# A hybrid decoder layer on one core: the second norm in pairs of d tiles, the gate's first chunk fed pair by pair, the last norm on VectorE, and a smaller gather rate in the first half of the u product

## The chip, the cores and the metric

The kernel runs on one core of one Trainium2 chip. The metric is the device time of one execution in microseconds (us). Engines are named as in the profile: PE is TensorE, DVE is VectorE, ACT is ScalarE, POOL is GpSimd and SP is SyncE, which here only issues DMAs.

## The reference

One decoder layer with 256 tokens of 2048 columns: attention, an expert layer (PEER) that fetches 16 single-neuron experts for each of 8 heads of a token, and a gated embedding. Three layer norms follow the three residual sums. What bears on the change:

```python
def peer_ffn(x, wq, sub_keys, u, v):
    ...
        ub = u[eb]                                   # u, v: 16384 experts x 2048
        vbk = v[eb]
        act = gelu(einsum('thed,td->the', ub, xb))
        w = gb * act
        return einsum('the,thed->td', w, vbk)
...
x = layer_norm(alpha * x + mix_out, ln_g[i, 0], ln_b[i, 0])
ffn_out = peer_ffn(x, ...)
x = layer_norm(alpha * x + ffn_out, ln_g[i, 1], ln_b[i, 1])     # "second norm"
gate = sigmoid(einsum('bsd,de->bse', x, ple_gate[i]))           # 2048 x 2048
emb = einsum('bsk,kd->bsd', p[i], ple_proj[i])
x = layer_norm(alpha * x + gate * emb, ln_g[i, 2], ln_b[i, 2])  # "last norm"
```

## The kernel before, in words

**The expert layer.** 256 tokens are cut in two kinds. For 156 of them (`NDT`) the products with u and v run densely on TensorE over all 16384 experts, 128 blocks `ia` of 128 experts, each a weight load `wf` of 1 MB on SyncE's queue with `WF = 5` buffers. For the other 100 (`NSP`) the chosen rows are gathered: `gb` tiles of 128 rows by 2048 floats, fetched by indirect DMAs on GpSimd's queue (100 of `u_rows`, then 100 of `v_rows`) and used by VectorE (L841, L851). Dense blocks and gathers run side by side. `gathers(rate)` adds `rate` to a sum at every block and, for each whole one, issues one gather: a `mark` (a tiny DMA on SyncE's queue, L871, between the weight loads), a copy of it on GpSimd (`pace`, L872), and the gather (L874). So a gather can't start before the weight loads that stand ahead of its mark. The rates are `GU` for the first 64 blocks of u, `GUG` for the other 64, and `GV`, `GVG` for the two passes of v over halves of d (`dh` 0 and 1). What is left over of the 200 gathers is issued at the rate `GV` in the second pass of v, as long as there are any. `v` goes block by block in 16 matmuls.

**The gate stage** begins when the residual sums are transposed back (`res2`) and the statistics of both token tiles t (128 tokens each) are known (`stats2`, with rstd a power on GpSimd, L483). x2 is normalized, transposed in 128 x 128 tiles on TensorE (`ps_x2T`), multiplied by gain and bias per d tile on the way out of PSUM (`ln_cols`: even d tiles on VectorE, odd ones on ScalarE), and split in a high part (ScalarE's copy, L518) and a low part (VectorE's subtraction, L519), since a float32 product is made of three reduced ones: `mm3` (L222, L223, L224) is hi x wh, hi x wl, lo x wh. The weights `ple_gate` come in four chunks c of 512 columns, each as four loads, and are split in the same way, `wh` on ScalarE (L115) and `wl` on VectorE (L116), 16 pairs of 512 columns for a chunk: `parts0` (the first 8 pairs of chunk 0, split early) and `gate_parts`.

Before: `ln2(t)` normalizes all of a token tile, 512 columns at a time, alternating between VectorE (L1208) and ScalarE (L1206), then transposes four d tiles and makes X2 of `LB = 2` of them (128 columns of one token tile each). Token tile 0 is done whole, then half of tile 1, then the rest. The first chunk of the gate runs over the first half of d for both token tiles, then over the second.

`gate_out(c, t, ...)` takes a finished chunk: `em` (loaded by GpSimd's queue), sigmoid (L1234), times `em` (L1235), added to alpha x2 (L1236), and statistics (L1239). `natural_x2(c)` gives x2 its gain and bias in rows (loads of ln_g and ln_b, then two operations for each token tile on GpSimd, L1269 and L1270). `finish(t)` is the last norm: two passes over the columns on VectorE (L1247, L1255), with the last 448 or 320 columns on ScalarE and GpSimd (L1250 to L1252), each slice stored as it is done.

What sets the order: the Tile framework schedules the program and inserts the waits; instructions wrapped in `keep` hold the order in which they were written on their engine. Every engine works through its queue in that order, and a waiting instruction holds up what stands behind it.

Of the kernel before, what the change touches and what calls it, by code (L numbers as in the profile page):

```python
# [54 lines left out]
GU, GUG = 0.64, 0.75  # L55
# [8 lines left out]
LB = 2  # L64
# [99 lines left out]
def build(tc, a, out):  # L164
# [15 lines left out]
    half_neg = c0p.tile([P, 1], F32, name="half_neg")  # L180

# [37 lines left out]
    def mm3(ps, xt, k, t, wh, wl, start, stop):  # L219
        hi = xt[:, k, t * P:(t + 1) * P]  # L220
        lo = xt[:, k, T + t * P:T + (t + 1) * P]
        nc.tensor.matmul(ps, hi, wh, start=start, stop=False)  # L222
        nc.tensor.matmul(ps, hi, wl, start=False, stop=False)  # L223
        nc.tensor.matmul(ps, lo, wh, start=False, stop=stop)  # L224
# [276 lines left out]
    def ln_cols(dst, which, ps, d0, nd, n):  # L501

        for j in range(nd):
            dt = d0 + j
            g, b = gT[:, which, dt:dt + 1], bT[:, which, dt:dt + 1]
            if j % 2:
                nc.scalar.activation(dst[:, j, :], ps[:, j * n:(j + 1) * n], AF.Identity, bias=b,
                                     scale=g)
            else:
                nc.vector.tensor_scalar(dst[:, j, :], ps[:, j * n:(j + 1) * n], g, b,  # L510
                                        op0=ALU.mult, op1=ALU.add)

    def ln_T(pool, which, ps, d0, nd, c0, n):

        xx = pool.tile([P, nd, n], F32, name="ln_xx", tag="ln_xx", bufs=3)
        ln_cols(xx, which, ps, d0, nd, n)
        hi = X2[:, d0:d0 + nd, c0:c0 + n]
        nc.scalar.copy(hi, xx)  # L518
        return nc.vector.tensor_tensor(X2[:, d0:d0 + nd, T + c0:T + c0 + n], xx, hi.bitcast(F32),  # L519
                                       op=ALU.subtract)  # L520
# [679 lines left out]
    def ln2(t, d4s=range(ND // 4)):  # L1200
        if 0 in d4s:
            mv, rstd, nmr = stats2[t]
            for c in range(NCH):
                s = slice(c * 512, (c + 1) * 512)
                if c % 2:
                    nc.scalar.activation(x2[t][:, s], x2[t][:, s], AF.Identity, bias=nmr, scale=rstd)  # L1206
                else:
                    nc.vector.tensor_scalar(x2[t][:, s], x2[t][:, s], mv[:, 0:1], rstd,  # L1208
                                            op0=ALU.subtract, op1=ALU.mult)
        for d4 in d4s:  # L1210
            ps = pbank(pp, "ps_x2T")
            for j in range(4):
                dt = 4 * d4 + j
                nc.tensor.transpose(ps[:, j * P:(j + 1) * P], x2[t][:, dt * P:(dt + 1) * P], ident)
            for j in range(0, 4, LB):
                last = ln_T(l2, 1, ps[:, j * P:(j + LB) * P], 4 * d4 + j, LB, t * P, P)
        return last
# [8 lines left out]
    def gate_out(c, t, ps, c0, n):  # L1226
# [11 lines left out]
        for j in range(c0, c0 + n, 256):  # L1238
            nc.vector.bn_stats(st3[t][:, 2 * c + j // 256, :],  # L1239
                               x2[t][:, c * 512 + j:c * 512 + j + 256])  # L1240

    def finish(t, gr3, br3):
        mv, rstd, nmr = ln_stats(l2, st3[t], True)
        cut = [0, 512, 1024, D - (320 if t else 448), D]
        cs = [slice(*p_) for p_ in zip(cut, cut[1:])]
        for s in cs[:-1]:
            nc.vector.scalar_tensor_tensor(x2[t][:, s], x2[t][:, s], mv[:, 0:1], gr3[:, s],  # L1247
                                           op0=ALU.subtract, op1=ALU.mult)
        s = cs[-1]
# [163 lines left out]
```

## Time and profile before

| | |
|---|---|
| device time, median of 3 runs | 1786.87 us (1785.68 to 1787.45) |
| the profiled execution's own time | 1785.93 us |
| its span | 1784.2 us |
| granted TensorE clock | 0.998 |
| TensorE / VectorE / ScalarE / GpSimd busy | 98 / 60 / 31 / 30% |
| data moved | 606.23 MB, mean 340 GB/s |
| first half of u | about 532 to 806 us |
| statistics of the second norm | 1673 us |
| first and last gate matmul | 1679 and 1772 us |

Times in the profile are from the start of the span. A row of a group names line, engine, operation, the tiles (out<-in), shapes and count, then busy time, mean ns of one, and the idle time of the engine before them with what ended it. A row of a timeline gives the start, the length, and in brackets the engine's idle time before it with its releaser. A window gives for each engine the busy time in a stretch and the count of instructions. Some matmul records are missing from a trace.

### The profile page before, as it was taken

The page shows a single profiled execution, that of the slowest core. Times are in us where ns is not written, and L with a number is a line of the kernel's source. Part 1 is how long each engine was busy: PE and PEld are TensorE (multiplying, and loading weights), DVE is VectorE, ACT ScalarE, POOL GpSimd, SP SyncE. Part 2 cuts the span into 40 slices and gives each one's busy share as a digit, 9 for nine tenths or more (in the row PEclk, how much of TensorE's full clock was granted, in tenths as well). Part 3 has the DMA queues.
Part 4 walks back from the last instruction along what each step waited for, and adds up shares of the span by engine and source line. Part 5 has one row for each costly group of instructions (what it writes and reads, how often), then busy time and mean ns, then how long its engine had stood idle before and what let it go on. Part 6 is the DMA issues. An engine that isn't in the chain of part 4 may idle for free.

```text
span 1784.2 us, 30408 instructions
## 1 busy us (share of the span) xinstructions
PE 1755.0 (98%) x12074; PEld 1646.9 (92%) x12074; DVE 1064.5 (60%) x1706; ACT 546.5 (31%) x1363; POOL 530.9 (30%) x576
## 2 busy tenths in 40 slices
PE   8999999999999999999999999999999999999997
PEld 6888888888889999999999999999999999999786
DVE  5555589654698868455555544966433334333777
ACT  5677478733110100103333313652000000000552
POOL 0133033105346227232233332323233323220232
PEclk9999999999999999999999999999999999999999
DMA  7544644567998999999999999999999999998481
GB/s 283 191 165 166 235 143 154 195 239 253 381 418 311 421 416 416 421 421 419 420 419 410 418 419 413 404 418 399 421 421 420 421 421 420 416 411 341 167 298 65
DMA packets 99695, 606.23 MB, mean 340 GB/s; under 512 B 12824, under 2 KB 14672, under 8 KB 35648
## 3 DMA queue, kind: packets, MB, share of 16 engines
q1 hardware_dynamic: 67792, 387.91, 55.0%
q0 software_dynamic: 30320, 213.62, 29.3%
q10 hardware_dynamic: 1440, 2.75, 0.4%
q8 instruction: 95, 1.56, 0.4%
q14 instruction: 48, 0.39, 0.1%
HBM read 598.36 MB, written 6.03 MB: 339 GB/s over the span
## 4 chain that ended last, share of the span: by engine, by line
PE 89%; DMA 8%; DVE 2%; ACT 1%; issue 0%; SPq 0%; DVEq 0%; ACTq 0%
PE ps_v L1053 30%; PE ps_u L215 26%; PE ps_qk L203 7%; PE ps_q L215 6%; DMA wf<-peer_u 5%; PE ps_qk L205 3%; PE ps_v L223 2%; PE ps_v L224 2%; PE ps_v L222 2%; PE ps_gate L223 1%; PE ps_gate L222 1%; PE ps_gate L224 1%; PE ps_mix L223 1%; PE ps_mix L224 1%; PE ps_mix L222 1%; DMA wf<-peer_v 1%
## 5 line engine op out<-in xcount | busy, mean ns | idle before, releaser
L1053 PE MATMUL ps_v<-A,wf 128*128 128x156 f32 x4096 | 551.9, 297 | 0.8 <-DMA wf<-peer_v 0.8
L1053 PEld LDWEIGHTS ps_v<-A,wf 128*128 128x128 f32 x4096 | 544.5, 190 | 1.8 <-DMA wf<-peer_v 1.3
L215 PE MATMUL ps_u<-XF,wf 128*128 128x156 f32 x3904 | 531.5, 297 | 5.9 <-DMA wf<-peer_u 4.5
L215 PEld LDWEIGHTS ps_u<-XF,wf 128*128 128x128 f32 x3904 | 519.6, 190 | 10.0 <-ACT A L986 5.6
L851 DVE SCALAR_TENSOR_TENSOR y<-gb,ew,y 128x2048 f32<-128x2048 f32 x94 | 220.8, 2349 | 222.0 <-DMA gb<-v_rows,eig 221.8
L841 DVE SCALAR_TENSOR_TENSOR gb<-gb,xq 128x2048 f32<-128x2048 f32 x100 | 231.5, 2319 | 147.7 <-DMA gb<-u_rows,eig 147.7
L116 DVE TENSOR_TENSOR wl<-wf,wh 128x1024 fp32r<-128x1024 f32 (+1 forms) x199 | 213.3, 1095 | 99.0 <-ACT wh L115 97.2
L872 POOL COPY pace<-mark 1x1 f32<-1x1 f32 x200 | 116.4, 582 | 513.9 <-DMA mark<-c_iota 513.4
L115 ACT CAST wh<-wf 128x1024 fp32r<-128x1024 f32 (+1 forms) x199 | 171.8, 893 | 151.3 <-PE ps_yn L897 39.8
L203 PE MATMUL ps_qk<-X,wh 128*128 128x512 f32 x512 | 185.2, 401 | 0.0
L986 ACT ACTIVATE A<-ps_u 128x156 f32<-128x156 f32 x128 | 38.4, 300 | 442.9 <-PE ps_u L215 357.0
L874 POOL DMA_INDIRECT gb<-u_rows,eig x100 | 114.7, 1147 | 143.7 <-DVE gb L841 74.7
L874 POOL DMA_INDIRECT gb<-v_rows,eig x100 | 123.4, 1234 | 78.4 <-DVE y L851 39.0
L205 PE MATMUL ps_qk<-X,wl 128*128 128x256 f32 x512 | 145.7, 285 | 0.0
L939 ACT ACTIVATE hi<-eq,ghf 128x64 f16<-128x64 f16 x312 | 104.5, 335 | 40.6 <-DVE eq L933 35.9
L203 PEld LDWEIGHTS ps_qk<-X,wh 128*128 128x128 f32 x512 | 96.4, 188 | 21.9 <-issue 1.0
L215 PE MATMUL ps_q<-XF,wf 128*128 128x256 f32 x512 | 113.6, 379 | 0.6 <-DVE XF L510 0.6
L1114 ACT COPY x<-ps_y 128x256 f32<-128x256 f32 (+3 forms) x12 | 5.2, 439 | 350.0 <-DVE st L1113 349.8
L215 PEld LDWEIGHTS ps_q<-XF,wf 128*128 128x128 f32 x512 | 95.9, 190 | 13.1 <-DVE XF L510 0.8
L940 ACT ACTIVATE lo<-eq,glf 128x64 f16<-128x64 f16 x312 | 104.1, 334 | 0.0
L205 PEld LDWEIGHTS ps_qk<-X,wl 128*128 128x128 f32 x512 | 96.3, 188 | 2.5 <-issue 1.3
L957 DVE SCALAR_TENSOR_TENSOR A<-ps_G,A 128x30 f32<-128x30 f32 (+2 forms) x96 | 32.6, 368 | 38.0 <-PE ps_G L947 21.9
(261 smaller groups left out, 1836.1 us busy)
## 6 DMA issues: line engine op xcount, KB each, us to landing
wf<-peer_v SPq DMA_DIRECT2D x128, 1024.0 KB
wf<-peer_u SPq DMA_DIRECT2D x122, 1024.0 KB
wf<-w_qk SPq DMA_DIRECT2D x64, 512.0 KB
wf<-w_out SPq DMA_DIRECT2D x32, 512.0 KB
wf<-peer_wq SPq DMA_DIRECT2D x16, 1024.0 KB
wf<-ple_gate SPq DMA_DIRECT2D x16, 1024.0 KB
wf<-w_v SPq DMA_DIRECT2D x31, 512.0 KB
early<-peer_u SPq DMA_DIRECT2D x6, 1024.0 KB
```

Source lines behind the costliest of these rows:

```text
L115: self.order(nc.scalar.copy(wh, src))
L116: self.order(nc.vector.tensor_tensor(wl, src, wh.bitcast(F32), op=ALU.subtract))
L203: nc.tensor.matmul(ps, wh[:, j * P:(j + 1) * P], xt[:, dt, :], start=dt == 0, stop=False)
L205: nc.tensor.matmul(ps[:, :T], wl[:, j * P:(j + 1) * P], xt[:, dt, :T], start=False, stop=dt == ND - 1)
L215: nc.tensor.matmul(ps[:, :T - t0], wf[:, dt * P:(dt + 1) * P], xt[:, dt, t0:], start=dt == 0, stop=dt == ND - 1)
L841: keep(nc.vector.scalar_tensor_tensor(g, g, 1.0, xq[i], op0=ALU.mult, op1=ALU.mult, accum_out=eact[i][:, j:j + 1]))
L851: keep(nc.vector.scalar_tensor_tensor(ys[i], g, ew[i][:, j:j + 1], ys[i], op0=ALU.mult, op1=ALU.add))
L872: keep(nc.gpsimd.tensor_copy(pace, mark))
L874: keep(nc.gpsimd.indirect_dma_start(out=g, out_offset=None, in_=a[kind], in_offset=bass.IndirectOffsetOnAxis(ap=eig[i][:, 0, j:j + 1], axi ...
L939: nc.scalar.mul(hi[:, j, :], eq[:, j, :], ghf[:, t])
L940: nc.scalar.mul(lo[:, j, :], eq[:, j, :], glf[:, t])
L1053: return nc.tensor.matmul(ps[:, (j % 2) * NDT:(j % 2 + 1) * NDT], vf[:, j * P:(j + 1) * P], W_of(ia), start=False, stop=ia == NIA - 1 and ...
```

## The change

Four things are edited.

1. `GU` goes from 0.64 to 0.60.
2. The second norm: `ln2_norm(c)` normalizes 512 columns of token tile 0 on VectorE and of token tile 1 on ScalarE. `ln2_pair(d2)` transposes two d tiles for both token tiles (four transposes in one PSUM bank) and makes X2 of 256 columns for each. All of it is wrapped in `keep`.
3. The gate's first chunk: for each pair of d tiles, the norm if the pair is even, the pair's X2, up to two weight splits, then the twelve matmuls of the pair before (`gate_pair`). `natural_x2(0)` with its loads stands behind `pace2`, a copy on GpSimd that reads X2 of d tile 13. The first eight splits of chunk 1 are written ahead of the last pair's matmuls.
4. The last norm: all columns on VectorE, in slices of 512 for token tile 0 and of 640, 640, 512 and 256 for token tile 1; token tile 0's is written ahead of the last half chunk's output. All stores are issued by SyncE.

```diff
-GU, GUG = 0.64, 0.75
+GU, GUG = 0.60, 0.75
...
-    def ln2(t, d4s=range(ND // 4)):
...
+    def ln2_norm(c):
+        s = slice(c * 512, (c + 1) * 512)
+        (mv, rstd, _), (_, rstd1, nmr1) = stats2
+        keep(nc.vector.tensor_scalar(x2[0][:, s], x2[0][:, s], mv[:, 0:1], rstd,
+                                     op0=ALU.subtract, op1=ALU.mult))
+        keep(nc.scalar.activation(x2[1][:, s], x2[1][:, s], AF.Identity, bias=nmr1, scale=rstd1))
+
+    def ln2_pair(d2):
+        d = slice(2 * d2, 2 * d2 + 2)
+        ps = pbank(pp, "ps_x2T")
+        for j in range(2):
+            for t in range(NT):
+                c0 = (2 * d2 + j) * P
+                keep(nc.tensor.transpose(ps[:, j * T + t * P:j * T + (t + 1) * P],
+                                         x2[t][:, c0:c0 + P], ident))
+        xx = l2.tile([P, 2, T], F32, name="ln_xx", tag="ln_xx", bufs=2)
+        ln_cols(xx, 1, ps, 2 * d2, 2, T, keep)
+        hi = X2[:, d, :T]
+        keep(nc.scalar.copy(hi, xx))
+        keep(nc.vector.tensor_tensor(X2[:, d, T:], xx, hi.bitcast(F32), op=ALU.subtract))
...
+    def finish(t, mv, rstd, cut):
+        cs = [slice(*p_) for p_ in zip([0] + cut, cut + [D])]
+        for s in cs:
+            keep(nc.vector.scalar_tensor_tensor(x2[t][:, s], x2[t][:, s], mv[:, 0:1], gr3[:, s],
+                                                op0=ALU.subtract, op1=ALU.mult))
+        for s in cs:
+            keep(nc.vector.scalar_tensor_tensor(x2[t][:, s], x2[t][:, s], rstd, br3[:, s],
+                                                op0=ALU.mult, op1=ALU.add))
             nc.sync.dma_start(out[t * P:(t + 1) * P, s], x2[t][:, s])
-
-    ln2(0)
-    ln2(1, range(ND // 8))
...
-    parts = [parts0, gate_parts(0, 1)]
-    ln2(1, range(ND // 8, ND // 4))
+    gw = [sg.load(a["ple_gate"][0, i]) for i in range(2, 4)]
+    pss = [pbank(pa, "ps_gate") for _ in range(NT)]
+
+    def gate_pair(d2):
+        for k in range(2 * d2, 2 * d2 + 2):
+            for t in range(NT):
+                mm3(pss[t], X2, k, t, *parts0[k], k == 0, k == ND - 1, keep)
+
+    for d2 in range(ND // 2):
+        if d2 % 2 == 0:
+            ln2_norm(d2 // 2)
+        ln2_pair(d2)
+        if d2 > 1 and len(parts0) < ND:
+            parts0.append(sg.split(gw[(len(parts0) - 8) // 4], len(parts0) % 4 * 512))
+        if d2 > 3 and len(parts0) < ND:
+            parts0.append(sg.split(gw[(len(parts0) - 8) // 4], len(parts0) % 4 * 512))
+        if d2 > 0:
+            gate_pair(d2 - 1)
+    keep(nc.gpsimd.tensor_copy(pace2, X2.bitcast(F32)[0:1, ND - 3, 0:1]))
+    natural_x2(0, nc.gpsimd)
     for t in range(NT):
         keep(nc.scalar.copy(em3[:, t], pse[t]))
-    pss = [pbank(pa, "ps_gate") for _ in range(NT)]
-    for half in range(2):
-        for t in range(NT):
-            gate_mm(pss[t], t, parts[half], 0, 512, half * ND // 2)
-        if not half:
-            natural_x2(0, nc.gpsimd)
+    first = gate_parts(1, 0)
+    gate_pair(ND // 2 - 1)
     for c in range(NCH):
         if c == NCH - 1:
+            finish(0, *mr0, [512, 1024, 1536])
             gate_out(c, 1, ps_half, 256, 256)
+            finish(1, *finish_stats(1), [640, 1280, 1792])
             break
         gate_out(c, 0, pss[0], 0, 512)
-        first = gate_parts(c + 1, 0)
+        if c:
+            first = gate_parts(c + 1, 0)
         gate_out(c, 1, pss[1], 0, 512)
         parts = first + gate_parts(c + 1, 1)
         natural_x2(c + 1, nc.sync)
...
         gate_out(c + 1, 0, pss[0], 0, 512)
+        mr0 = finish_stats(0)
         gate_out(c + 1, 1, pss[1][:, :256], 0, 256)
         ps_half = pss[2][:, :256]
-    for t in range(NT):
-        finish(t, gr3, br3)
```

More of the change, by code (lines that the diff above doesn't have):

```diff
@@ L63 @@
 WF = 5
-LB = 2
 class Pools:
@@ L180, in build @@
     half_neg = c0p.tile([P, 1], F32, name="half_neg")
+    pace2 = c0p.tile([1, 1], F32, name="pace2")
     xap = pools.open("xap", "left", bufs=1)
@@ L506, in ln_cols @@
             if j % 2:
-                nc.scalar.activation(dst[:, j, :], ps[:, j * n:(j + 1) * n], AF.Identity, bias=b,
-                                     scale=g)
-            else:
[L510 to L520, printed above, removed]
+                order(nc.scalar.activation(dst[:, j, :], ps[:, j * n:(j + 1) * n], AF.Identity,
+                                           bias=b, scale=g))
+            else:
+                order(nc.vector.tensor_scalar(dst[:, j, :], ps[:, j * n:(j + 1) * n], g, b,
+                                              op0=ALU.mult, op1=ALU.add))
     def ln_rows(pool, which):
```

56 lines of the change are left out of this document (16 added, 40 removed).

## The prediction

> **What bounds the kernel now.** I read the page first, then windows of the first half of the u product, then GpSimd's timeline there, then the groups and timelines of the last 115 us. The page:
>
> ```profile
> PE 1755.0 (98%) x12074; PEld 1646.9 (92%) x12074; DVE 1064.5 (60%) x1706; ACT 546.5 (31%) x1363; POOL 530.9 (30%) x576
> PE 89%; DMA 8%; DVE 2%; ACT 1%; issue 0%; SPq 0%; DVEq 0%; ACTq 0%
> ```
>
> TensorE is busy 98% of the span, and the chain that ends last is TensorE for 89% and a DMA for 8%. So only two kinds of time can move: the few microseconds in which TensorE waits, and what follows its last matmul. A reader should not take the other engines' shares as slack: in the gate stage they set when TensorE starts.
>
> Windows of two views (stretch, length, then busy time and count for each engine, granted clock, DMA share, GB/s):
>
> ```profile
> core 0: us, PE busy (x) PEld busy (x) DVE busy (x) ACT busy (x) POOL busy (x), PEclk, DMA share, GB/s
> 600.00:620.00 20.00, 20.00 (x153) 20.00 (x152) 17.94 (x58) 1.60 (x6) 5.03 (x8) 1.00 1.01 419
> 620.00:650.00 30.00, 29.37 (x214) 28.29 (x214) 15.91 (x44) 2.10 (x7) 7.02 (x9) 1.00 1.02 414
> 720.00:770.00 50.00, 46.76 (x341) 45.00 (x340) 22.57 (x26) 7.27 (x18) 13.90 (x15) 1.00 1.01 421
> 795.00:806.00 11.00, 10.32 (x76) 9.91 (x75) 8.37 (x11) 2.08 (x9) 2.11 (x3) 1.00 1.02 424
> 840.00:860.00 20.00, 18.74 (x151) 18.07 (x150) 14.01 (x20) 8.24 (x34) 7.17 (x9) 1.00 1.02 422
> 1606.00:1636.00 30.00, 30.00 (x228) 30.00 (x228) 14.54 (x13) 3.74 (x7) 3.50 (x4) 1.00 0.98 393
> 1636.00:1656.00 20.00, 20.00 (x141) 18.93 (x140) 4.39 (x9) 2.18 (x4) 0.00 (x0) 1.00 0.62 216
> ```
>
> An unstalled u stretch runs 152 or 153 matmuls in 20 us, 0.132 us each; a u block has 32 of these records, 4.2 us. By that pace the four u windows lack 14, 39, 8 and (by idle time) about 10 matmuls: 1.8, 5.1, 1.0 and 1.3 us. The DMA share is 1 in all of them: TensorE waits there because a weight load shares full DMA engines with expert gathers. At 421 GB/s one load, 1.05 MB, takes 2.5 us; a gather (128 rows of 2048 floats) has the same size.
>
> ```profile
> 723.85 0.96 POOL L874 DMA_INDIRECT gb<-u_rows,eig  x1 [4.61 <-DVE gb L841]
> 738.78 0.96 POOL L874 DMA_INDIRECT gb<-u_rows,eig  x1 [3.83 <-DVE gb L841]
> 741.11 0.18 POOL L872 COPY pace<-mark 1x1 f32<-1x1 f32 x1 [1.37 <-DMA mark<-c_iota]
> ```
> ```profile
> L874 POOL DMA_INDIRECT gb<-v_rows,eig x100: 956/958/3097, 1020.0 to 1613.8; - x100
> ...
> DMA to landing us min/median/max: 5.5/12.3/22.5
> ```
>
> Until 739 GpSimd issues a gather every 4.98 us (the first and the last of four stand here) and waits for VectorE to free a buffer, not for a mark: it works off a backlog of marks. At 741 it waits for a mark for the first time, so only from there does GU set the rate.
>
> **Fewer gathers (GU 0.64 to 0.60).** Over the 64 u blocks of the first half 2.56 gathers go, 6.4 us of DMA time. In the new order of SyncE's queue one mark fewer has been issued by block 20 to 26, and two by block 45 (about 725 us). The first stall (620 to 650) falls into the backlog, where marks do not count: it stays. In the window from 720 to 770 TensorE got 39 matmuls too few, 1.2 blocks at 32 matmuls, so 1.2 loads or 3 us of DMA time; two gathers fewer give 5. I take that stall and the one at 795 as nearly gone: -5.5 of 6.1 us. Bounds: -1.5 (the backlog only shortens and the loads gain no turn before 750) and -8 (the stall at 840 goes too, and some of the first). The 2.56 gathers come later, behind the last v gather, which was issued at 1613.8: v makes 0.35 of a gather for every 16 matmuls (2.1 us), so they take 7.3 such steps, 15.5 us; the last is issued about 1629 and lands, at the median of 12.3, about 1641. The DMA share is 0.98 to 1636 and 0.62 behind it, which takes them: +0.3, up to +2 if the last of them hold up the residual sums in which they are added.
>
> **The gate's first chunk.** Its durations, from the groups of 1672 to 1785 and from the two lines of `ln_cols` (min/median/max ns, the 256-column form is the one after the change):
>
> ```profile
> L222 PE MATMUL ps_gate<-wh,X 128*128 128x512 f32 x112 | 43.4, 393 | 3.4 <-ACT X L518 3.4
> L116 DVE TENSOR_TENSOR wl<-wf,wh 128x512 fp32r<-128x512 f32 x56 | 35.2, 697 | 0.1
> L115 ACT CAST wh<-wf 128x512 fp32r<-128x512 f32 x56 | 29.8, 619 | 0.0
> L1270 POOL TENSOR_TENSOR x<-x,XF 128x512 f32<-128x512 f32 x8 | 13.2, 1673 | 0.0
> L1269 POOL TENSOR_TENSOR x<-x,XF 128x512 f32<-128x512 f32 x8 | 10.3, 1308 | 44.6 <-DMA XF<-ln_g 44.6
> ...
> L1234 ACT ACTIVATE sig<-ps_gate 128x512 f32<-128x512 f32 x7 | 4.2, 599 | 33.5 <-PE ps_gate L224 33.5
> L1206 ACT ACTIVATE x<-x,ln_nmr,ln_rstd 128x512 f32<-128x512 f32 x4 | 3.0, 807 | 0.1
> L1208 DVE TENSOR_SCALAR x<-x,ln_mv,ln_rstd 128x512 f32<-128x512 f32 x4 | 2.0, 551 | 0.6 <-POOL ln_rstd L483 0.6
> ```
> ```profile
> L510 DVE TENSOR_SCALAR XF<-ps_x1T,gT,bT x8: 534/535/546, 411.2 to 418.7; 128x256 f32<-128x256 f32 x8
> L507 ACT ACTIVATE XF<-ps_x1T,bT,gT x8: 556/564/598, 412.8 to 419.2; 128x256 f32<-128x256 f32 x8
> ```
> ```profile
> 1673.92 1.19 POOL L483 TENSOR_TENSOR ln_rstd<-ln_rstd,half_neg 128x1 f32<-128x1 f32 x2 [59.19 <-DVE ln_rstd L482]
> ```
> ```profile
> 1679.53 0.60 PE L1214 MATMUL ps_x2T<-ident,x 128*128 128x128 f32 x4
> ```
> ```profile
> 1705.36 0.59 ACT L1234 ACTIVATE sig<-ps_gate 128x512 f32<-128x512 f32 x1
> ...
> 1727.55 0.60 ACT L1234 ACTIVATE sig<-ps_gate 128x512 f32<-128x512 f32 x1 [1.45 <-PE ps_gate L224]
> ```
>
> The last three fences are of GpSimd's, TensorE's and ScalarE's timelines. The sigmoids at 1705.36 and 1727.55 mark the ends of chunks 0 and 1: 22.2 us for 96 matmuls, so one costs 0.2275 and chunk 1 now loses 0.35. A pair of d tiles has 12 matmuls, 2.73 us, and four transposes, 0.60 from the first to the last result and so 0.11 each in the pipeline, 0.44: 3.17 us of TensorE. Its chain on the other engines is serial, since the program lets ScalarE's half of `ln_cols` wait for VectorE's and the copy for both: the transposes and the hand-over 0.64, then 0.58, 0.60, 0.66 and 0.62, each a row above with 0.04 for the hand-over or less its overlap with what follows. The program puts the next norm behind all that on both engines, behind the weight splits of the pair too, and TensorE's queue has the transposes of every second pair waiting for that norm, with 12 matmuls of the pair before standing behind them. So from the transposes of an even pair to those of the next: 3.17 + 0.64 + 2.46, plus 0.62 for each weight split, plus 0.59 for the norm: 7.5 us with one split, 8.1 to 8.6 with two, against 6.34 of TensorE.
>
> In numbers: both rstd by 1675.11, the norm of token tile 1 on ScalarE (0.29 and 0.81) done by 1676.3, transposes 1676.4, X of pair 0 ready 1678.9. Its matmuls end 1681.8; the norm for pairs 2 and 3 ends 1682.5 (stall 0.6); next transposes at 1690.0 (stall 1.1) and 1698.3 (1.9); then 0.44 + 0.44 + 3 x 2.73 of work and 0.4 for the pipeline: chunk 0 ends about 1707.7 instead of 1705.3. So **+2.4**. It keeps the first wait and trades the other of the two that make up the 3.4 us of L222 for three smaller ones. Bounds: -1.6 (nothing but the first wait), +5.5 (each split delays the norm by both engines' rows).
>
> **Chunk 1.** `natural_x2(0)` moves from the start of the stage to behind `pace2`, which waits for ScalarE's copy of pair 6. On GpSimd's queue the loads of `em` for chunk 0 stand behind it.
>
> ```profile
> 1686.56 1.14 POOL L1230 DMA_DIRECT2D em<-s_emb  x2
> ```
> ```profile
> 1709.75 0.68 DVE L1235 TENSOR_TENSOR sig<-sig,em 128x512 f32<-128x512 f32 x1
> 1710.53 0.69 DVE L1236 SCALAR_TENSOR_TENSOR x<-x,sig 128x512 f32<-128x512 f32 x1
> 1711.26 0.75 DVE L1239 BATCH_NORM_STATS2 st<-x 128x6 f32<-128x256 f32 x2
> ...
> 1721.99 1.79 DVE L1235 TENSOR_TENSOR sig<-sig,em 128x512 f32<-128x512 f32 x1 [5.18 <-ACT sig L1234]
> ```
> ```profile
> em<-s_emb POOLq DMA_DIRECT2D x6, 256.0 KB, 3.5
> ...
> XF<-ln_g POOLq DMA_DIRECT2D x1, 256.0 KB, 5.9
> ```
>
> Copy of pair 6 at 1700.8, pace 0.5, ln_g issued 1701.3, landed 5.9 later: 1707.2. Four operations of 1.31 and 1.67 each twice: 1713.2. `em` issued there, landed 3.5 later: 1716.7. On VectorE the two outputs of chunk 0 now stand between the first and the second eight splits of chunk 1: wl of tile 8 comes after 2 x (0.69 + 0.69 + 0.75) = 4.3, with 0.7 of its own at 1721.7. TensorE needs it 49 matmuls into chunk 1, at 1718.9. That is 2.8 us of stall; the GpSimd operations of `natural_x2(1)` now run in the same stretch, and one VectorE operation beside such a one took 1.79 instead of 0.68. I add half a meeting: **+3.3**. Bounds: 0 (both loads land in half the time) and 7 (all four meet).
>
> The Trainium skill's page "SBUF — State Buffer", section "Who interferes with whom", says that VectorE and GpSimd take one shared port pair as an exclusive lock, for a whole instruction. By that rule up to four meetings, 4.4 us, would come on top of 2.8 here, 7.2 instead of 3.3; the row of 1.79 agrees with a wait of most of one GpSimd operation.
>
> **Chunk 2.** In the new order of TensorE the first token tile of chunk 1 ends 6 matmuls before the chunk does (1.36 us; 27, or 6.1 us, before). Its output now stands ahead of the splits of chunk 2 on both engines. Sigmoid 0.6, 0.69, 0.69, 0.75, a split 0.7 and two hand-overs make 3.5; less 1.36 and one matmul, TensorE stands 1.9 us. With half a meeting with GpSimd: **+2.5**, bounds 1.9 and 4. Chunk 3 keeps 28 matmuls of distance: nothing. The 0.35 that chunk 1 loses now is part of these: -0.35.
>
> **Tail.**
>
> ```profile
> 1772.00 0.38 ACT L1234 ACTIVATE sig<-ps_gate 128x256 f32<-128x256 f32 x1 [3.63 <-PE ps_gate L224]
> ```
> ```profile
> 1773.16 0.41 DVE L1235 TENSOR_TENSOR sig<-sig,XF 128x256 f32<-128x256 f32 x1
> ...
> 1775.06 2.27 DVE L1247 SCALAR_TENSOR_TENSOR x<-x,ln_mv,g_row 128x512 f32<-128x512 f32 x3
> 1777.24 3.47 DVE L1255 SCALAR_TENSOR_TENSOR x<-x,ln_rstd,b_row 128x512 f32<-128x512 f32 x3
> ```
>
> VectorE starts the last product 1.2 us behind the last matmul and ends 8.7 behind it. After: it has eight passes of 512 for tile 0 instead of six, free of GpSimd. The first token tile of chunk 3 now ends 72 short matmuls ahead of the last, 8.5 us at 0.118; its output, the statistics and the first half of tile 1's output take 5.1 of these, so the passes start 3.4 ahead of the last matmul and 8 x 0.66 ends 1.9 behind it. Then 1.9 to the passes as now, and twice 2048 columns at 2.27/1728 us per column, 5.4: 9.2 in all, +0.5; the last store has 256 columns and lands some 0.3 to 0.5 earlier. **0**, bounds -0.7 and +1.
>
> **Sum.** 2.4 + 3.3 + 2.5 - 0.35 = +7.9 in the gate; -5.5 in u; +0.3 in v: +2.7. The profiled execution took 1785.93 (span 1784.2), so 1788.6 by its own time; the median of the runs shown, 1786.87, lies 0.9 above it, so **1789.5**. A difference of 0.2%, 3.6 us, is about what a measurement of this kernel can tell from none: 1783.3 to 1790.4 counts as the same.
>
> **Rivals.**
> (a) The gate runs at TensorE's pace: the norms do get done between the splits, and chunk 1 meets no late `em`. Its place is chunk 0's wait at every even pair; it decides if the chain of a pair with norm and splits is under 6.34 us instead of 7.5. Then the gate gives -1.6 and the whole -1.6 - 5.5 + 0.3: 1780, faster. Against it stand the rows of the chain; for it, that PE's total work is unchanged. Chance 0.15.
> (b) GpSimd's loads land sooner than the rows say: two of each alone, not beside weight loads. If ln_g and `em` together take 3.3 us less, chunk 1's stall is gone: 1786.2, no change. Chance 0.17.
> The page "DMA: Bandwidth & Descriptors" of the Trainium skill, section "Anatomy of one DMA — SWDGE (gpsimd) path", gives 2.0 us plus the bytes at 436 GB/s for a DMA on this path, an estimate of 2.6 us here. That would be 4.2 us less in the two landings; the rows of 5.9 and 3.5 speak against it in this stage.
> (c) The gathers free nothing: the loads' stall returns at the next place because the DMA engines stay full anyway. For it: the share is 1 in every window of u, and a transfer that is only moved does not leave the queue shorter. Then 1789.5 + 5.5 = 1795, slower. Chance 0.20.
> (d) The late gathers hold the last residual sums and the stage starts 3 us later: 1792.5. Chance 0.06.
> The forecast itself, 1786.5 to 1793, has 0.42.
>
> **How the numbers follow.** Leaving out most of (a) below and the far ends of (c) above, the range is 1781 to 1796. Faster: (a) 0.15 and the lower ends of forecast and (b), 0.07: 0.22. Same: most of (b) and the lower half of the forecast: 0.36. Slower: 0.42.
>
> **What would show it.** Right: u windows of 720 to 770 with 375 or more matmuls; three waits of ps_x2T for VectorE or ScalarE, growing; `em` landing after 1715; a wait of ps_gate L223 (the wl matmul) in the middle of chunk 1 and at the start of chunk 2. Wrong: the sigmoids of chunk ends 22 us apart, or the u window with 341 matmuls as now.

## The result and the profile after

The changed kernel takes 1798.07 us (median of 4 runs, 1796.77 to 1799.64), the kernel before 1787.16 beside it: ratio 1.0063, 95% interval 1.0045 to 1.0080. It is slower by some 11 us; the forecast was 1789.5 in a range from 1781 to 1796.

The profiled execution has a span of 1795.0 instead of 1784.2, 10.8 us more. From the starts of TensorE's matmuls in both traces the difference divides as follows. u goes from its first start to its last, the next stretch to the last start of the matmuls of `ps_emb`, behind which the second norm begins. A chunk of the gate is counted by 96 matmuls of 512 columns (two of 256 count as one), from its first start to the next chunk's.

| stretch | before | after | difference |
|---|---|---|---|
| up to the first u matmul | 531.79 | 532.84 | +1.05 |
| u | 567.17 | 560.42 | -6.75 |
| v, residual sums, statistics | 575.52 | 577.11 | +1.59 |
| to the first gate matmul | 4.47 | 4.27 | -0.20 |
| gate chunk 0 | 25.95 | 29.28 | +3.33 |
| gate chunk 1 | 22.45 | 28.35 | +5.90 |
| gate chunk 2 | 21.98 | 27.36 | +5.38 |
| gate chunk 3 | 22.36 | 22.42 | +0.06 |
| last start of a matmul to the end of the span | 12.47 | 12.95 | +0.48 |

Nothing ahead of u is edited; its 1.05 is how executions differ (u starts between 531.8 and 534.8 in the fourteen traces of this case). So u gains what was forecast and a little more, and the gate stage loses 14.5 us instead of 7.9.

TensorE's waits (tile and line, what it waited for: us in all, times, longest), two rows of the kernel before and then the changed kernel, whose line numbers differ (its L115 is the kernel before's L116):

```profile
PE ps_u L215 <- DMA wf<-peer_u: 4.5, 13, 0.5
PE ps_gate L222 <- ACT X L518: 3.4, 2, 1.7
```
```profile
PE ps_gate L223 <- DVE wl L115: 6.9, 4, 3.3
...
PE ps_x2T L1206 <- DVE x L1195: 3.4, 3, 2.0
PE ps_v L1044 <- DMA wf<-peer_v: 2.3, 3, 1.0
PE ps_gate L222 <- ACT X L1211: 1.4, 1, 1.4
PE ps_u L215 <- DMA wf<-peer_u: 1.2, 3, 0.5
```

Before, the gate's matmuls waited 3.4 us, all in chunk 0 and for X. Now the largest group is a wait for `wl`, VectorE's half of the weight split, and waits for loads of `peer_u` fell from 4.5 to 1.2. The windows of u and two in the gate stage (PE busy and count first; the last three columns are clock, DMA share and GB/s):

```profile
620.00:650.00 30.00, 29.24 (x213) 28.08 (x212) 17.03 (x46) 1.81 (x6) 7.44 (x10) 1.00 1.02 414
720.00:770.00 50.00, 48.90 (x366) 48.20 (x365) 18.76 (x22) 7.16 (x18) 10.72 (x13) 1.00 1.01 420
795.00:806.00 11.00, 11.00 (x91) 10.97 (x91) 5.49 (x9) 3.49 (x15) 3.00 (x5) 1.00 1.02 419
840.00:860.00 20.00, 20.00 (x176) 19.96 (x175) 10.55 (x15) 7.05 (x31) 7.88 (x7) 1.00 1.01 419
...
1712.00:1720.00 8.00, 6.98 (x21) 4.67 (x21) 7.76 (x9) 0.38 (x1) 5.72 (x5) 0.79 0.62 204
1738.00:1746.00 8.00, 8.00 (x29) 6.31 (x29) 7.86 (x15) 2.50 (x5) 0.00 (x0) 0.80 0.87 312
```

The first stall stays (213 matmuls against 214), the window from 720 to 770 has 366 matmuls instead of 341, the stalls at 795 and 840 are gone. In the last two windows the granted clock falls to 0.8, which it did nowhere in the kernel before between the first matmul of u and the last of the gate.

Where the time of chunk 1 goes is read from VectorE's and GpSimd's timelines side by side (start, length, count; the line's idle time and releaser in brackets), and from the landing of the two loads of `em` that GpSimd issues at 1709.2. VectorE:

```profile
1697.72 1.29 DVE L115 TENSOR_TENSOR wl<-wf,wh 128x512 fp32r<-128x512 f32 x2
...
1702.24 13.34 DVE L115 TENSOR_TENSOR wl<-wf,wh 128x512 fp32r<-128x512 f32 x8 [0.80 <-ACT wh L114]
1715.51 1.76 DVE L1230 TENSOR_TENSOR sig<-sig,em 128x512 f32<-128x512 f32 x1
...
1720.94 4.89 DVE L115 TENSOR_TENSOR wl<-wf,wh 128x512 fp32r<-128x512 f32 x8
1731.74 1.11 DVE L1230 TENSOR_TENSOR sig<-sig,em 128x512 f32<-128x512 f32 x1 [5.91 <-ACT sig L1229]
1732.96 1.58 DVE L1231 SCALAR_TENSOR_TENSOR x<-x,sig 128x512 f32<-128x512 f32 x1
1734.57 0.75 DVE L1234 BATCH_NORM_STATS2 st<-x 128x6 f32<-128x256 f32 x2
1735.24 5.18 DVE L115 TENSOR_TENSOR wl<-wf,wh 128x512 fp32r<-128x512 f32 x8
```

GpSimd:

```profile
1697.14 0.71 POOL L1285 COPY pace<-X 1x1 f32<-1x1 f32 x1 [26.16 <-ACT X L1211]
1697.80 0.63 POOL L1260 DMA_DIRECT2D XF<-ln_g  x1
...
1702.40 1.70 POOL L1262 TENSOR_TENSOR x<-x,XF 128x512 f32<-128x512 f32 x1 [3.40 <-DMA XF<-ln_g]
...
1709.19 1.14 POOL L1225 DMA_DIRECT2D em<-s_emb  x2
1710.34 1.29 POOL L1262 TENSOR_TENSOR x<-x,XF 128x512 f32<-128x512 f32 x1
...
1715.11 1.61 POOL L1263 TENSOR_TENSOR x<-x,XF 128x512 f32<-128x512 f32 x1
```

The loads of `em` (view of the tile from 1709 to 1710), and TensorE's wait for `wl` of tile 8, the first of the second eight splits, 50 matmuls into chunk 1:

```profile
DMA to landing us min/median/max: 5.1/5.1/5.1
```
```profile
1721.67 0.50 PE L223 MATMUL ps_gate<-wl,X 128*128 128x512 f32 x1 [1.51 <-DVE wl L115]
```

The eight operations of the natural rows of chunks 0 and 1 run from 1702.4 to 1716.7, one behind the other. In the same stretch VectorE makes the first eight splits of chunk 1, and they take 13.3 us: the first, begun before GpSimd, takes 0.69 us, the other seven 1.77 to 2.48 each. The next eight, with GpSimd idle, take 4.9 together. `sig` times `em` then starts at 1715.5 with no idle time before it: `em`, issued at 1709.2, had landed at 1714.3 and was not waited for, but by only 1.3 us.

### The profile page after: what moved, and what is told of

It reads as the page before. It is cut to its first block, busy times and chain, and to the rows that moved or that the text cites. A ratio compares the mean times of both kernels' runs of the same rounds, so it can differ in the third digit from the quotient of the medians.

```text
span 1795.0 us, 30354 instructions
## 1 busy us (share of the span) xinstructions
PE 1759.3 (98%) x12074; PEld 1648.1 (92%) x12074; DVE 1065.3 (59%) x1692; ACT 541.6 (30%) x1343; POOL 535.2 (30%) x573
## 3 DMA queue, kind: packets, MB, share of 16 engines
q0 software_dynamic: 30320, 213.62, 29.2%
## 5 line engine op out<-in xcount | busy, mean ns | idle before, releaser
L115 DVE TENSOR_TENSOR wl<-wf,wh 128x1024 fp32r<-128x1024 f32 (+1 forms) x199 | 220.9, 1131 | 110.8 <-ACT wh L114 99.0
L863 POOL COPY pace<-mark 1x1 f32<-1x1 f32 x200 | 107.0, 535 | 517.1 <-DMA mark<-c_iota 516.5
L865 POOL DMA_INDIRECT gb<-u_rows,eig x100 | 127.5, 1275 | 129.6 <-DVE gb L832 68.7
L215 PEld LDWEIGHTS ps_q<-XF,wf 128*128 128x128 f32 x512 | 95.9, 190 | 13.1 <-DVE XF L510 0.8
L223 PE MATMUL ps_gate<-wl,X 128*128 128x512 f32 (+1 forms) x144 | 54.2, 381 | 6.9 <-DVE wl L115 6.9
```

Of the source, the lines that this page charges most:

```text
L115: self.order(nc.vector.tensor_tensor(wl, src, wh.bitcast(F32), op=ALU.subtract))
L215: nc.tensor.matmul(ps[:, :T - t0], wf[:, dt * P:(dt + 1) * P], xt[:, dt, t0:], start=dt == 0, stop=dt == ND - 1)
L863: keep(nc.gpsimd.tensor_copy(pace, mark))
L865: keep(nc.gpsimd.indirect_dma_start(out=g, out_offset=None, in_=a[kind], in_offset=bass.IndirectOffsetOnAxis(ap=eig[i][:, 0, j:j + 1], axi ...
```

## The experiments

Each run stands beside runs of the kernel before on the same chip; the table has the medians and the ratios, and the chunk times are counted as above. Kernels are compared by what each lies above or below its own before: the changed kernel +10.9.

| run | us | before | ratio (95%) | chunks 0, 1, 2, 3 | half clock in the gate, us (chunk) |
|---|---|---|---|---|---|
| changed kernel | 1798.07 | 1787.16 | 1.0063 (1.0045 to 1.0080) | 29.3, 28.4, 27.4, 22.4 | 3.4 (1), 3.4 (2) |
| GU alone | 1780.43 | 1786.16 | 0.9971 (0.9960 to 0.9983) | 25.9, 22.5, 22.0, 22.4 | none |
| all but GU | 1805.59 | 1786.16 | 1.0119 (1.0102 to 1.0136) | 29.3, 28.3, 28.3, 22.4 | 6.8 (1), 6.8 (2) |
| no natural rows in 0 and 1 | 1789.93 | 1786.16 | 1.0024 (1.0013 to 1.0036) | 29.3, 22.1, 23.4, 22.4 | none |
| no pace2 | 1793.18 | 1786.16 | 1.0043 (1.0027 to 1.0060) | 34.6, 22.1, 22.8, 22.4 | 6.8 (0) |
| norms ahead | 1796.82 | 1785.91 | 1.0070 (1.0053 to 1.0087) | 27.8, 28.2, 27.2, 22.4 | 3.4 (0), 3.4 (2) |
| splits ahead | 1791.70 | 1785.91 | 1.0035 (1.0022 to 1.0047) | 29.2, 27.7, 22.1, 22.4 | none |
| no natural rows in 1 | 1796.51 | 1785.91 | 1.0068 (1.0051 to 1.0085) | 31.5, 24.0, 28.4, 22.4 | 6.8 (0), 6.8 (2) |
| last norm alone | 1787.00 | 1785.91 | 1.0008 (0.9998 to 1.0018) | 25.7, 22.5, 22.0, 22.4 | none |
| norms and splits ahead, no pace2 | 1790.23 | 1785.52 | 1.0023 (1.0013 to 1.0033) | 32.9, 22.5, 22.1, 22.4 | 6.8 (0) |
| norms and splits ahead | 1788.24 | 1785.52 | 1.0015 (1.0006 to 1.0025) | 26.7, 29.3, 22.1, 22.4 | 3.4 (1) |
| the same, rows 1 to 3 held | 1799.30 | 1786.23 | 1.0075 (1.0058 to 1.0091) | 26.7, 26.5, 25.0, 29.9 | 3.4 (1), 6.8 (3) |
| GU 0.56 alone | 1788.34 | 1786.23 | 1.0010 (1.0000 to 1.0019) | 25.8, 22.3, 22.0, 23.1 | none |

The chunk times are those of one traced execution of each kernel. The last column says how long TensorE's granted clock was 0.5 in it during the gate, and in which chunk: a matmul then starts 0.427 us behind the one before instead of 0.2275, so 3.4 us of it cost 1.6 us of TensorE's time, unless TensorE would have waited for something else anyway. Differences of one or two us between chunk times are to be read with it.

**GU alone**, in the kernel before.

```diff
-GU, GUG = 0.64, 0.75
+GU, GUG = 0.60, 0.75
```

> The kernel before with GU at 0.60 and nothing else. Theory A (the u and v parts of the changed kernel's trace are GU's doing and the gate stage is separate): u ends some 6 us earlier, v gives back some 1.5 by the gathers moved behind it, and the time is about 5 us lower, 1782; the gate stage keeps its 92.7 us from first to last gate matmul. Rival B (the gain in u came from elsewhere or is eaten in the gate stage, where loads now collide): within 1.5 us of before.

5.7 us faster, and the gate stage keeps 92.8 us: u takes 559.5 instead of 567.2, and v with what follows 575.4, so here it gives nothing back. Theory A holds but for v. This kernel beats both of the case.

**All but GU**: the changed kernel with 0.64.

```diff
-GU, GUG = 0.60, 0.75
+GU, GUG = 0.64, 0.75
```

> The changed kernel with GU back at 0.64. Theory A: u and v as before, the gate stage as in the changed kernel (107.4 us from first to last gate matmul), so some 5 us above the changed kernel: 1803. Rival B (part of the longer gate stage comes from late gathers or loads): chunks 0 to 2 shorter than 29.3, 28.4 and 27.4 us, and less than 1803.

19.4 above the kernel before, 8.5 more than the changed kernel and not 5. The gate takes 108.3 us, and u and v are those of before (566.9 and 575.8): with the old rate the gate is no shorter, so late gathers have no share in it, and rival B falls. Of the 8.5, the profile has 5.1 in u and v together, 0.9 in the gate and 1.7 in the tail. The tail hangs on the scheduler's order of chunk 3's matmuls, which differs between these programs: here the first token tile ends 59 short matmuls ahead of the last (7.1 us) instead of 72 (8.7), so its last norm starts later. In all four traces with 59 the span ends 14.3 to 14.6 us behind the last matmul's start, in those with 69 or more 12.5 to 13.1.

**No natural rows in chunks 0 and 1**, in the changed kernel.

```diff
-        for t in range(NT):
+        for t in range(NT if c > 1 else 0):
             keep(nc.gpsimd.tensor_tensor(x2[t][:, s], x2[t][:, s], gb[:, 0], op=ALU.mult))
```

> The changed kernel without GpSimd's eight operations of the natural rows of chunks 0 and 1 (gain and bias of x2 are left out for the first 1024 columns; loads and order stay). Theory A (the splits of chunk 1 are held up by these operations one by one, 13.3 us for eight instead of 5.0): the eight splits take 5 us again, chunk 1 takes 22.4 to 23 us instead of 28.4, and TensorE's clock stays full there; the time falls by 5.5 to 6.5 us, to about 1792. Rival C, the prediction's own (the two outputs stand between the splits and wait for late em loads): em still lands 3.5 us after its issue and the splits of tile 8 stay late; chunk 1 stays above 25 us.

VectorE's timeline there:

```profile
1703.11 4.91 DVE L115 TENSOR_TENSOR wl<-wf,wh 128x512 fp32r<-128x512 f32 x8 [0.80 <-ACT wh L114]
1709.02 0.69 DVE L1230 TENSOR_TENSOR sig<-sig,em 128x512 f32<-128x512 f32 x1 [1.00 <-DMA em<-s_emb]
```

It lies 3.8 above its before, 7.1 us better than the changed kernel. Eight splits take 4.9 us, chunk 1 22.1, though the outputs still stand between the splits and this time `em` is waited for, 1.0 us. So GpSimd's eight operations cost chunk 1 its 5.9 us, and rival C falls as it was written (chunk 1 above 25). But the run does not tell the slow splits from a late `em`: without the four operations of chunk 0 ahead of them on GpSimd's queue, the loads of `em` are issued 24.3 us behind the first gate matmul instead of 34.6. The run without the rows of chunk 1, below, keeps them late. Chunk 2 falls too, to 23.4, which was not expected: in this program the first token tile of chunk 1 ends 16 matmuls before the chunk instead of 6, and its output comes earlier. So the scheduler's order of TensorE's matmuls has a share in chunk 2.

**No pace2**: the copy is left out, so the first rows start early.

```diff
-    keep(nc.gpsimd.tensor_copy(pace2, X2.bitcast(F32)[0:1, ND - 3, 0:1]))
```

> The changed kernel without the copy to pace2, so that GpSimd starts the natural rows of chunk 0 as soon as the transposes that read x2 are done, and those of chunk 1 some 15 us later. Theory A: the eight operations fall beside chunk 0's chain instead of chunk 1's splits: chunk 1 22.4 to 24 us instead of 28.4, chunk 0 longer by 1 to 4 than 29.3, in sum 2 to 4 us faster than the changed kernel. Rival C: chunk 1 falls because em comes early, and chunk 0 is not touched: 6 us faster.

+7.0, 3.9 us better than the changed kernel. Chunk 1 falls to 22.1, chunk 0 rises by 5.3 us, more than the 1 to 4 expected. GpSimd's operations meet a split of 1.77 and one of 1.78 us there, and TensorE's waits in the chunk grow by 2.3 us; the rest is two stretches at half clock. The meeting is moved, not removed; rival C would have left chunk 0 alone. Chunks 0 and 1 together fall by only 0.9 us in the trace. The larger gain is in chunk 2, 22.8 instead of 27.4, which was not expected: here, too, the first token tile of chunk 1 ends 16 matmuls before the chunk.

**Norms ahead.**

```diff
-        if d2 % 2 == 0:
-            ln2_norm(d2 // 2)
+        if d2 == 0:
+            ln2_norm(0)
+        if d2 % 2 and d2 < ND // 2 - 1:
+            ln2_norm(d2 // 2 + 1)
         ln2_pair(d2)
```

> The changed kernel with the norm of the next 512 columns written ahead of the odd pair's X2 and of its weight splits, so that the transposes of an even pair don't wait for them. Theory A (chunk 0 is longer because those norms stand behind the splits on both engines): the three waits of 0.5, 1.1 and 2.2 us go, chunk 0 takes 25.5 to 27 us instead of 29.3; chunks 1 and 2 stay at 27 to 28.5, since what holds them is elsewhere; 2.5 to 3.5 us faster than the changed kernel. Rival D (the serial chain of a pair itself is the limit, wherever the norm stands): chunk 0 stays above 28.

TensorE's waits there:

```profile
PE ps_gate L223 <- DVE wl L115: 8.5, 4, 3.2
...
PE ps_gate L222 <- ACT X L1211: 1.8, 2, 1.4
PE ps_x2T L1206 <- ACT x L1197: 0.8, 1, 0.8
```

The three waits of the transposes for VectorE's norm (3.4 us) are gone, and chunk 0 falls by 1.5 to 27.8; the expected 25.5 to 27 is missed. A stretch at half clock (0.57 granted from 1674 to 1678) can have taken part of the gain. The time doesn't move (+10.9). The gate takes 105.6 us instead of 107.4, though the wait for `wl` grows from 6.9 to 8.5; but this program, too, is one of those with 59 short matmuls, and its tail is 14.3 us instead of 13.0. Most of the gain is given back there.

**Splits ahead**: chunks 2 and 3.

```diff
-        gate_out(c, 0, pss[0], 0, 512)
         if c:
             first = gate_parts(c + 1, 0)
+        gate_out(c, 0, pss[0], 0, 512)
```

> The changed kernel with the first eight weight splits of chunks 2 and 3 written ahead of the first output of the chunk before (sigmoid, product, sum, statistics). Theory A for chunk 2 (its first low part stands behind that output, which ends late): the wait of 3.4 us at its start goes and with it the stretch at half clock, chunk 2 takes 22 to 23.5 us instead of 27.4; chunk 1 stays at 28. The time falls by about 4 to 5 us. Rival E (the lock alone: GpSimd's operations of the next natural rows hold the splits wherever they stand): chunk 2 stays above 25.

Chunk 2 takes 22.1 us, chunk 1 27.7, and the run lies 5.8 above its before, 5.1 us better. GpSimd's operations of chunk 2 still run, now beside the outputs. Theory A holds for chunk 2, rival E falls.

**No natural rows in chunk 1 alone.**

```diff
-        for t in range(NT):
+        for t in range(0 if c == 1 else NT):
             keep(nc.gpsimd.tensor_tensor(x2[t][:, s], x2[t][:, s], gb[:, 0], op=ALU.mult))
```

> The changed kernel without GpSimd's four operations of the natural rows of chunk 1 alone (gain and bias are left out for columns 512 to 1023); those of chunk 0 stay. Theory A with a price by the piece (each GpSimd operation beside the splits costs VectorE about 1.05 us): eight splits take 4.9 + 4 x 1.05 = 9.1 us instead of 13.3, and chunk 1 takes 23 to 24.5 us instead of 28.4. Rival (the first GpSimd operations alone make the wait, or the wait is for em): chunk 1 stays above 26.

VectorE's timeline and three windows of this run:

```profile
1702.88 8.55 DVE L115 TENSOR_TENSOR wl<-wf,wh 128x512 fp32r<-128x512 f32 x8 [0.80 <-ACT wh L114]
1713.19 0.69 DVE L1230 TENSOR_TENSOR sig<-sig,em 128x512 f32<-128x512 f32 x1 [1.77 <-DMA em<-s_emb]
```
```profile
1673.00:1677.00 4.00, 3.62 (x9) 2.62 (x10) 2.30 (x4) 2.22 (x4) 0.00 (x0) 0.58 0.17 68
1695.00:1698.00 3.00, 3.00 (x10) 2.34 (x10) 1.51 (x3) 2.19 (x4) 0.94 (x2) 0.58 0.23 55
1733.00:1739.00 6.00, 6.00 (x15) 4.76 (x16) 5.93 (x11) 4.08 (x8) 0.43 (x1) 0.54 0.95 348
```

Four operations, 8.55 us: (8.55 - 4.91) / 4 = 0.91 us each, and (13.34 - 4.91) / 8 = 1.05 with eight. The price by the piece holds roughly, and chunk 1 takes 24.0. `em` landed as late as in the changed kernel (39.7 us behind the first gate matmul, there 39.6); the splits, done at 38.0 instead of 40.9, no longer hid it, and VectorE waited 1.8 us for it. So the slow splits were what came last in the changed kernel, with the late `em` close behind, and `em` takes over when they are shortened. The total hardly falls (+10.6). In the trace, TensorE's clock was near half speed in three stretches, two of them in chunk 0, and chunks 0 and 1 together fall by 2.2 us, not 4.3.

**Last norm alone**, in the kernel before: `finish_stats` and `finish` of the change and their places.

```diff
+            finish(0, *mr0, [512, 1024, 1536])
             gate_out(c, 1, ps_half, 256, 256)
+            finish(1, *finish_stats(1), [640, 1280, 1792])
             break
...
-    for t in range(NT):
-        finish(t, gr3, br3)
```

> The kernel before with the last norm of the changed kernel (all on VectorE, stores from SyncE, token tile 0 ahead of the last half chunk's output) and nothing else. The prediction's tail: 0, from -0.7 to +1; the changed kernel's trace says +0.4 behind the last matmul. Expected: within 1 us of before, VectorE ending 8.9 to 9.3 us behind the last matmul instead of 8.7. Rival F (the split over three engines was worth it): 2 us or more slower.

1.1 us above, with an interval that just takes in no change; the end lies 12.7 us behind the last matmul's start instead of 12.5. Rival F falls.

**Norms and splits ahead**, without and with the copy to pace2 (the diffs of three runs above together).

> The changed kernel with the three edits that were tried alone: norms ahead of the odd pair's X2, first splits ahead of the output, no copy to pace2. Theory A (chunk 0: norms behind splits; chunk 1: GpSimd's operations beside the splits; chunk 2: output ahead of the splits): chunk 0 27 to 31 us, since the eight operations now run beside it, chunks 1 and 2 22 to 23, together 96 to 99 us from first to last gate matmul instead of 107.4, so 1787 to 1790. The gate stage of before, 92.7, is not reached. Rival G (the pair-wise first chunk has no further cost once the three waits are gone): 93 us or less, and with GU's part 1781.

> As the run before, but with the copy to pace2. Theory A: chunk 0 26.5 to 28, chunk 1 28 (the operations are back beside its splits), chunk 2 22 to 23: 99 to 102 us, 1791 to 1793, some 3 us above the run without the copy. Rival G': the place of GpSimd's operations doesn't matter any more once norms and splits stand ahead: chunk 1 below 25.

The norms' gain shows in the second run: chunk 0 26.7. In the first, chunk 0 takes 32.9, above the 27 to 31 expected, and the sum is 100, not 96 to 99: GpSimd's operations stand beside chunk 0, and two stretches at half clock in it cost up to 3 us. In the second, chunk 1 takes 29.3, since the meeting is back at its splits (12.25 us for eight); 1.6 us of it is half clock. The expected order of the two is wrong: with the copy (+2.7) is 2 us faster than without (+4.7), not 3 slower. The two traces, 100.6 and 100.0 us of gate, do not show why. Either way some 7.5 us of the 14.5 remain, and both are slower than the kernel before even with GU's gain in them: rivals G and G' fall.

**The natural rows of chunks 1 to 3 held** behind the last split of their chunk, in the kernel with norms and splits ahead. The main lines:

```diff
+        if hold is not None:
+            keep(nc.gpsimd.tensor_copy(pace2, hold.bitcast(F32)[0:1, 0:1]))
         for t in range(NT):
...
+        hold = parts[-1][1]
+        natural_x2(c + 1, nc.sync, hold)
```

> As the run with the norms and the first splits ahead and the copy to pace2 kept, and GpSimd's natural rows of chunks 1 to 3 held by a copy that reads the last weight split of that chunk, so that only the four operations of chunk 0 can meet the splits of chunk 1. Theory A (price by the piece): eight splits 8.5 us instead of 12.3, chunk 1 23.5 to 24.5 us instead of 29.3, chunk 0 26.7 and chunk 2 22 as there; about 95 us from first to last gate matmul and 1783 to 1785. Rival (moving GpSimd's operations only moves the meeting to the output behind the splits): chunk 2 rises above 24.

VectorE's timeline:

```profile
1700.09 9.34 DVE L115 TENSOR_TENSOR wl<-wf,wh 128x512 fp32r<-128x512 f32 x8 [0.80 <-ACT wh L114]
1711.38 0.69 DVE L1230 TENSOR_TENSOR sig<-sig,em 128x512 f32<-128x512 f32 x1 [1.95 <-DMA em<-s_emb]
...
1737.76 0.69 DVE L1230 TENSOR_TENSOR sig<-sig,em 128x512 f32<-128x512 f32 x1 [12.32 <-DMA em<-s_emb]
```

My expectation of 1783 to 1785 failed by 15 us. The splits fell to 9.3, but in chunk 1 VectorE then waited 2.0 us for `em`, and the chunk took 26.5, not 23.5 to 24.5, 1.6 of it at half clock. Behind that, the loads of `em` stand behind the held copy on GpSimd's queue, and VectorE sat idle for 12.3 us until they landed: the mechanism that the prediction had put into chunk 1 of the change, here as the wait that ends last. Chunk 2 took 25.0, above the rival's 24, but not for its reason: GpSimd's four operations took 1.29 or 1.30 us each and met nothing, and TensorE waited 2.5 us for the splits behind that late output.

**GU 0.56 alone.**

```diff
-GU, GUG = 0.64, 0.75
+GU, GUG = 0.56, 0.75
```

> The kernel before with GU at 0.56. With 0.60 alone, u keeps 0.9 us of waits for loads, of which the first part lies in the backlog. Theory A (what is left does not hang on GU): no more than 1 us lower than with 0.60, so 1779.5 to 1782 beside a before of 1786; v may give back up to 1.5. Rival (each gather moved is worth 2.5 us of loads, as the bound of the prediction's sum has it): 4 us lower, 1776.

Neither: 1788.3. u falls by another 1.2 us (558.3), but v and what follows take 584.3 instead of 575.4. TensorE's waits there:

```profile
PE ps_v L1053 <- DMA wf<-peer_v: 6.1, 4, 4.4
...
PE ps_u L215 <- DMA wf<-peer_u: 1.2, 3, 0.5
```

With GU at 0.60 alone, the waits for loads of `peer_v` were 0.7 us. The gathers that u no longer makes are issued at the end of v (the last at 1628.1, before 1613.8), and TensorE then waits 4.4 us for a weight load at 1645; that the gathers hold this load is argued, not shown. Behind the wait TensorE ran at half clock for 6.8 us, which cost up to 3 us more.

## Why the prediction was wrong

**u and v.** The two terms were -5.5 and +0.3, -5.2 in all. The trace has -6.75 and +1.59, -5.16, and GU alone -5.7 in the time. The mechanism is right, and that the sum fits so closely is partly luck. The first stall stayed and that at 795 went, as forecast. From 720 to 770 there are 366 matmuls, not the 375 or more that it named as its sign, and the stall at 840, taken to stay, went. (Its count of lacking matmuls is rough in two windows: without a stall those from 795 and 840 hold 91 and 176, more than the 84 and 153 of its pace.) In v, 1.0 us of the 1.6 is one wait for a v load at 1645.7, not a wait in the residual sums. It is there in all nine traces with both GU 0.60 and the new gate stage (1.0 to 2.3 us), and in neither of the runs with one of them alone, so the late gathers do not make it by themselves; why the two together do is open. Rival (c) falls.

**Chunk 0.** +2.4, measured +3.3 less 0.2 for the first matmul. The serial chain, and the norms behind the splits, are as the prediction had them: the three waits are 0.4, 1.0 and 2.0 us (forecast 0.6, 1.1 and 1.9), and putting the norms ahead removes them. Rival (a) falls.

**Chunk 1: the step that failed.** The term was +3.3 - 0.35, and the trace has +5.9. The prediction let VectorE begin the outputs of chunk 0 as soon as `em` lands. It silently took the first eight splits of chunk 1 as done by then, and counted meetings with GpSimd for the four operations of the outputs alone. Since the stage began 4.3 us earlier than in the kernel before, its times and the measured ones are set side by side from the first gate matmul:

| us behind the first gate matmul | forecast | measured |
|---|---|---|
| `em` issued | 34.3 | 34.6 |
| `em` landed | 37.8 | 39.6 |
| first eight splits done | no term | 40.9 |
| outputs begin | 37.8 | 40.9 |
| `wl` of tile 8 done | 42.8 | 47.0 |
| TensorE needs it, at 0.2275 a matmul | 40.0 | 40.7 |

`em` came late as forecast, and 1.9 us later still, since it took 5.1 us to land and not 3.5. But it was not what VectorE waited for: the first eight splits, beside all but the last of GpSimd's eight operations, went on for 13.3 us instead of 4.9 and ended 1.3 us behind the landing. The outputs then took 5.4 us instead of 4.3, as one product met the last of these operations (1.76 us). So `wl` of tile 8 came 6.3 us behind TensorE's need instead of 2.8, or 3.3 with the half meeting that the prediction added, and that is nearly all that the chunk lost (28.35 against 21.84 at this pace). The waits of 1.4 and 0.7 us ahead of it, and the stretch at half clock from 1713.9, added little or nothing: TensorE still waited 1.5 us for tile 8. The run with the splits ahead has no half clock there and takes 27.7 against 28.4.

That GpSimd's operations are the cause of the whole is shown: without them chunk 1 takes 22.1. How it divides between the slow splits and the loads of `em` behind the same operations is read from the times above; with shorter splits `em` is waited for, as the run without the rows of chunk 1 shows. Rival (b), loads that land sooner, falls: ln_g took 4.4 and `em` 5.1 us, 9.5 together against 9.4 in the forecast.

The Trainium skill's rule that VectorE and GpSimd take a shared port pair as an exclusive lock ("SBUF — State Buffer", section "Who interferes with whom") agrees with the splits of 1.77 to 2.48 us instead of 0.69. The error was mine: I applied it to the outputs, not to every VectorE operation with two SBUF inputs in that stretch. That the 7.2 by this rule is nearer to the chunk's loss than 3.3 is luck, since it stood for four meetings of the outputs, of which one took place.

**Chunk 2: right mechanism, wrong size.** +2.5 forecast, +5.4 measured, and the run with the splits ahead takes all of it away. TensorE waited 3.3 us, not 1.9 to 2.5, since both two-input operations of the output met GpSimd (1.11 and 1.58 instead of 0.69). The rest is mostly the clock: from 1737.8 to 1741.2 the matmuls are 0.427 us apart instead of 0.2275, some 1.6 us lost, and nothing is waited for behind it. The prediction had no such term.

**Tail.** 0 forecast, +0.5 in the trace, and 1.1 us with an interval that takes in none in the run of it alone. Right; that a new order of chunk 3 could cost some 1.5 was not seen.

**The sum.** The gate was to lose 7.9 us and lost 14.5. Of the 6.6 between, chunk 1 has 3.0, chunk 2 2.9 and chunk 0 0.7.

## What to carry to other kernels

When an engine's work is moved, list every instruction that will run beside it in the new stretch, and all that stands behind it on its queue, not just those whose results are waited for: here eight elementwise operations on GpSimd made eight VectorE splits take 13.3 us instead of 4.9, and held back the loads of `em` behind them nearly as long. Removing one of two such delays uncovers the other. An engine's slack is per stretch, and a delayed start that is harmless by itself can make two such streams coincide. And a rate between two loads is worth tuning only up to where the work it pushes back finds room: 0.04 less gained 5.7 us, and 0.08 less gained nothing (2.1 us above, with an interval from none to 3.4).

## What the runs showed of the hardware that was not expected

TensorE's granted clock fell to half in the middle of busy work, for 3.41 us at a time or twice that, with matmuls 0.427 us apart, in the changed kernel 3 and 5 us behind the beginning of a wait. It took two stretches in the changed kernel, three in the run without the rows of chunk 1, none in the gate stage of the kernel before, whose two waits of 1.7 us stayed without it. Within one execution the stretches begin whole multiples of 3.41 us apart: 23.90 us in the changed kernel (7 times), 30.73 without pace2 (9 times), 20.48 and 37.55 without the rows of chunk 1 (6 and 11 times). So whether a wait is followed by half clock may hang on where it lies on that raster, which lies differently in each trace. The Trainium skill ("TensorE: Matmul & The Clock Gate", "Part 1: The HAM clock gate (the "warmup" mystery)") puts half speed behind an idle window of about 3.4 us that runs freely; the length and the raster of the stretches agree. A window of the changed kernel with its clock of 0.50, and TensorE's timeline at 1712:

```profile
1714.00:1716.00 2.00, 1.95 (x4) 1.13 (x5) 2.00 (x2) 0.00 (x0) 1.92 (x2) 0.50 0.03 12
```
```profile
1712.25 0.50 PE L223 MATMUL ps_gate<-wl,X 128*128 128x512 f32 x1 [1.40 <-DVE wl L115]
...
1713.94 0.79 PE L223 MATMUL ps_gate<-wl,X 128*128 128x512 f32 x1 [0.72 <-DVE wl L115]
1714.53 0.63 PE L224 MATMUL ps_gate<-wh,X 128*128 128x512 f32 x1
1714.96 0.63 PE L222 MATMUL ps_gate<-wh,X 128*128 128x512 f32 x1
...
1717.67 0.39 PE L222 MATMUL ps_gate<-wh,X 128*128 128x512 f32 x1
```

Here waits of 1.4 and 0.7 us with three matmuls between them stood ahead of it: one matmul takes 0.63 instead of 0.40 from the second wait on, and 0.39 again at 1717.67. TensorE was not idle throughout the 3.41 us ahead of the stretch but busy for 1.30 of them, by the profile. Where the Trainium skill's page has an idle window, these windows were partly busy, and the measurement decides. Of the 18 stretches at half clock between the start of u and the last gate matmul in all traces, none began behind 3.41 us in which TensorE was busy with matmuls other than transposes for more than 53%; but others no busier were not followed by one. Which waits trigger it is not settled by these runs.
